# Down projections of two thirds of each feed-forward layer by Strassen's algorithm

## The chip, the core and the metric

The kernel runs on one core of one Trainium2 chip. A core has a matrix engine (TensorE, "PE" in the profile; its weight loads are listed apart as "PEld"), three engines for elementwise work (VectorE "DVE", ScalarE "ACT", GpSimd "POOL") and a queue that issues most transfers (SyncE, "SP"). Each engine runs its instructions in the order of its own queue, and waits for the others by semaphores. TensorE multiplies a 128x128 block of weights that stands in its array (the stationary operand) with a moving operand of up to 512 columns and adds the result into a bank of the accumulation memory (PSUM), which VectorE and ScalarE read. The other tiles lie in the on-chip memory SBUF, with 128 partitions.

The metric is the device time of the whole program in microseconds (us).

## The reference, cut to what matters

The model is a small decoder: one sequence of 512 tokens with 1024 features goes through an attention mixer, a feed-forward layer, a state-space mixer, a second feed-forward layer and a last norm. Everything is in float32. The change concerns only the last product of the feed-forward layers, `@ w_down`, whose inner dimension D_FF is 2816 = 22 x 128.

```python
D_MODEL = 1024
SEQ = 512
D_FF = 2816
FFN_CONV = 3
...
def conv_ffn(h, w_up, conv_w, conv_b, w_down):
    u = causal_depthwise_conv(h @ w_up, conv_w, conv_b)
    gate, up = u[..., :D_FF], u[..., D_FF:]
    return (jax.nn.silu(gate) * up) @ w_down
...
def reference(x, ...):
    cos, sin = rope_tables(x.shape[1])
    for i in range(DEPTH):
        h = rmsnorm(x, mix_norm_w[i])
        ...
        h = rmsnorm(x, ffn_norm_w[i])
        x = x + conv_ffn(h, ffn_w_up[i], ffn_conv_w[i], ffn_conv_b[i], ffn_w_down[i])
    return rmsnorm(x, final_norm_w)
```

## The kernel before

**Layout.** Features lie on the partitions and tokens along the free dimension. The residual stream is eight tiles `xr[0..7]` of 128x512 (L588). Weights arrive by transfer as float32, in units of 128x1024: eight 128x128 blocks side by side.

**Products in three parts.** A float32 product is made of three faster ones. Each operand is split into a high part, the value cast to the type fp32r, and a low part, the rest. `load_unit` (L116) does this for a unit of weights: SP issues the transfer into a tile `raw` (4 of them in turn, pool `wr`), ScalarE casts it to `hi` (L125) and VectorE subtracts to get `lo` (L126); there are five `hi` and five `lo` in turn (pool `wh`). `mm3` (L136) issues high x high, high x low and low x high into one bank, by `long_product` (L133), which calls the matrix product with the columns in the order that `in_turns` (L129) gives. So a unit of 8 blocks is 24 products of 512 columns.

**A feed-forward layer** (`ffn`, L610) goes over the 22 hidden tiles c in three parts, `FF_PARTS = ((0, 8), (8, 8), (16, 6))`. For each c it projects two units, gate and up (`project`, L146: 24 products each, into one of three banks "mm"), VectorE multiplies by the norm's factor `rbc` (L620), `conv` (L602) applies the three taps (one instruction of ScalarE, L603, and two of VectorE, L605), ScalarE applies silu (L624), and GpSimd multiplies the two (L627). The result is split for the down projection: ScalarE casts `g_h` (L629), GpSimd subtracts `g_l` (L630). The tiles `g_h`, `g_l` come from `high_low` (L81), eight of each in turn, so that a part fills them.

At the end of a part `down` (L263) computes what the part's hidden tiles add to the eight output tiles: for each output tile m it loads a unit of `wdn`, multiplies its blocks with the part's `g` tiles, and `add` (L639) adds the bank to `xr[m]` on VectorE (L640). The product with the last `g` tile of a part is put off: that of m = 0 and m = 1 until three blocks into m = 2, then by one output tile (`late`, `depth`). So the down stage can start while the last `g` is still being made.

**Order.** A planner orders the instructions of each engine at build time by a simulated clock. Within a `manual_schedule` block the named engines keep the order in which the code issues; the down stages are in such a block for TensorE. The last part of layer 1 ends in `finish` (L1059), which also does the last norm; its last two output tiles are made in halves of 256 tokens (L1106 to L1117), so the old kernel has 72 products of 256 columns there.

**Other tiles that the change touches.** Banks: "mm" 3, "aux" 3, "side" 2, each 128x512. SBUF tiles in turn: "a" 13, "us" 3, "tmp" 2, "sq" 2, and, used by the state-space mixer only, "xdt" 2, "yt" 2, "lm" 4, "ee" 2, "prev" 2. `_layout` (L1176) arranges the weights on the host before the launch; `wdn` is one unit per layer, part and output tile.

## Time and profile before

| | |
|---|---|
| median of 3 runs | 1626.8 us (1625.71 to 1626.92) |
| the profiled execution, its own time | 1626.55 us |
| its span, first to last instruction | 1624.6 us |
| mean granted TensorE clock | 0.999 |
| moved by DMA | 165.13 MB, mean 102 GB/s |
| matrix products | 8038 |

The page lists busy time of each engine, then 40 equal slices of the span, the DMA queues, the chain of work that ended last (followed back from the last instruction to what released each step), the costliest groups of instructions, and the DMA issues. A group's row reads: line, engine, operation, written tile <- read tiles, shapes, count | busy us, mean ns of one | idle time of the engine just before them, and what ended it. A row of the timeline or of the chain begins with the start in us from the span's start and the duration in us. A row of a table by stretches has the stretch, its length, then busy us and instruction count of PE, PEld, DVE, ACT and POOL, the granted clock, the DMA share and GB/s.

The span divides into these stages, by the chain in order of time: attention until about 474 us, its output projection until 503, feed-forward layer 0 until 852, the state-space mixer until about 1268, feed-forward layer 1 until the end at 1624.6. In each feed-forward layer the three parts are visible as stretches of up projections ("u") and of down projections ("wd", in the very last one "wz").

### The profile page before, as it was taken

To read this page: it belongs to the slowest core of one execution; us is meant where nothing else is said; L and a number is where in the kernel's file an instruction comes from. 1 tells how busy PE (TensorE), PEld (TensorE's weight loads), DVE (VectorE), ACT (ScalarE), POOL (GpSimd) and SP (SyncE) were. 2 spreads that over 40 slices of the span, in tenths; PEclk is the share of its full clock that TensorE was granted. 3 is DMA by queue.
4 is the path that set the end of the run, shared out by engine and by line. 5 is a ranking of instruction groups with operands and counts; after the bars stand their busy time and mean duration, and the time that the engine had idled before them with its cause. 6 is when DMAs were issued, how large, how long until landed. Compare 5 with 4: busy or idle time off the path is not lost.

```text
span 1624.6 us, 21067 instructions
## 1 busy us (share of the span) xinstructions
PE 1615.7 (99%) x8038; PEld 1382.9 (85%) x8038; DVE 1082.8 (67%) x1813; ACT 655.0 (40%) x965; POOL 418.6 (26%) x272
## 2 busy tenths in 40 slices
PE   9999999999999999999999999999999999999998
PEld 8888888888888888888887888888888888888887
DVE  6366665266647855764657899988897784574564
ACT  5233332333334532432445455544443442342343
POOL 0444453045402320220231222222111341121020
PEclk9999999999999999999999999999999999999999
DMA  7322222222224323223233433334332232332321
GB/s 259 98 80 83 78 91 80 96 85 79 78 78 134 113 91 105 103 81 117 81 101 104 148 108 115 100 100 127 114 126 90 93 104 91 104 104 91 104 78 52
DMA packets 53235, 165.13 MB, mean 102 GB/s; under 512 B 6224, under 2 KB 9680, under 8 KB 53136
## 3 DMA queue, kind: packets, MB, share of 16 engines
q1 hardware_dynamic: 52304, 163.01, 30.5%
q8 instruction: 63, 1.03, 0.3%
q10 hardware_dynamic: 832, 0.79, 0.1%
q14 instruction: 36, 0.29, 0.1%
HBM read 161.62 MB, written 2.16 MB: 101 GB/s over the span
## 4 chain that ended last, share of the span: by engine, by line
PE 99%; ACT 0%; DVE 0%; POOL 0%; POOLq 0%; DVEq 0%; issue 0%
PE u L134 29%; PE qk L134 16%; PE wd L134 12%; PE v L134 8%; PE xs L134 5%; PE z L134 5%; PE wso L134 5%; PE wo L134 3%; PE c L134 3%; PE b L134 3%; PE wz L134 2%; PE py L830 1%; PE pg L490 1%; PE pp L477 1%; PE po L485 1%; PE pf L838 1%
## 5 line engine op out<-in xcount | busy, mean ns | idle before, releaser
L134 PE MATMUL u<-xh,lo_u 128*128 128x512 f32 x704 | 268.9, 382 | 0.0
L134 PE MATMUL u<-xh,hi_u 128*128 128x512 f32 x704 | 268.8, 382 | 0.0
L134 PE MATMUL u<-xl,hi_u 128*128 128x512 f32 x704 | 266.3, 378 | 0.0
L627 POOL TENSOR_TENSOR au<-au,au 128x512 f32<-128x512 f32 x43 | 58.5, 1360 | 422.2 <-DVE au L605 396.6
L605 DVE SCALAR_TENSOR_TENSOR au<-usu,par,au 128x511 f32<-128x511 f32 (+1 forms) x176 | 159.4, 911 | 7.6 <-ACT au L603 2.9
L125 ACT CAST hi_u<-raw_u 128x1024 fp32r<-128x1024 f32 x88 | 91.1, 1044 | 168.4 <-PE u L134 95.6
L388 POOL TENSOR_TENSOR rotqk<-rotqk,sr 32x512 f32<-32x512 f32 x48 | 88.2, 1837 | 250.2 <-DVE rotqk L387 239.8
L134 PEld LDWEIGHTS u<-xl,hi_u 128*128 128x128 f32 x704 | 131.7, 187 | 24.5
L134 PEld LDWEIGHTS u<-xh,lo_u 128*128 128x128 f32 x704 | 131.7, 187 | 24.0
L134 PEld LDWEIGHTS u<-xh,hi_u 128*128 128x128 f32 x704 | 131.7, 187 | 21.8 <-issue 0.4
L134 PE MATMUL qk<-xh,hi_qk 128*128 128x512 f32 x384 | 148.6, 387 | 0.0
L134 PE MATMUL qk<-xh,lo_qk 128*128 128x512 f32 x384 | 147.1, 383 | 0.0
L134 PE MATMUL qk<-xl,hi_qk 128*128 128x512 f32 x384 | 145.6, 379 | 0.0
L126 DVE TENSOR_TENSOR lo_u<-raw_u,hi_u 128x1024 fp32r<-128x1024 f32 x88 | 113.8, 1299 | 29.9 <-ACT hi_u L125 29.9
L620 DVE TENSOR_TENSOR usu<-u,rbc 128x512 f32<-128x512 f32 x88 | 60.3, 690 | 93.1 <-PE u L134 86.4
L640 DVE TENSOR_TENSOR xr<-xr,wd 128x512 f32<-128x512 f32 x40 | 27.3, 688 | 116.9 <-PE wd L134 116.9
L125 ACT CAST hi_qk<-raw_qk 128x1024 fp32r<-128x1024 f32 x48 | 50.3, 1047 | 130.3 <-PE qk L134 69.3
L134 PEld LDWEIGHTS qk<-xh,lo_qk 128*128 128x128 f32 x384 | 71.8, 187 | 13.3
L134 PEld LDWEIGHTS qk<-xl,hi_qk 128*128 128x128 f32 x384 | 71.9, 187 | 12.8
L389 POOL TENSOR_TENSOR qk<-qk,rotqk 32x512 f32<-32x512 f32 x48 | 81.5, 1698 | 3.8
L125 ACT CAST hi_wd<-raw_wd 128x1024 fp32r<-128x1024 f32 (+1 forms) x48 | 46.1, 972 | 88.7 <-PE wd L134 55.6
L134 PEld LDWEIGHTS qk<-xh,hi_qk 128*128 128x128 f32 x384 | 71.9, 187 | 11.2
(647 smaller groups left out, 3768.5 us busy)
## 6 DMA issues: line engine op xcount, KB each, us to landing
raw_u<-in_wup SPq DMA_DIRECT2D x88, 512.0 KB, 3.3
raw_qk<-in_wqk SPq DMA_DIRECT2D x48, 512.0 KB, 3.3
raw_wd<-in_wdn SPq DMA_DIRECT2D x32, 512.0 KB, 3.2
raw_xs<-in_win SPq DMA_DIRECT2D x16, 512.0 KB, 3.3
raw_z<-in_win SPq DMA_DIRECT2D x16, 512.0 KB, 3.4
lm<-rows SPq DMA_DIRECT2D x32, 256.0 KB, 5.4
raw_wso<-in_wso SPq DMA_DIRECT2D x16, 512.0 KB, 3.3
raw_v<-in_wv SPq DMA_DIRECT2D x12, 512.0 KB, 3.5
```

The costliest lines, as they stand in the source:

```text
L125: SC.copy(hi[:, s], raw[:, s])
L126: low.tensor_tensor(lo[:, s], raw[:, s], hi.bitcast(F32)[:, s], op=ALU.subtract)
L134: T.matmul(in_turns(dst), w, in_turns(x), start=first, stop=last)
L388: G.tensor_tensor(rot[R, :], rot[R, :], sr[R, :], op=ALU.mult)
L389: G.tensor_tensor(at(t)[R], at(t)[R], of(rot)[R], op=ALU.add)
L477: T.transpose(pp[:, b * P : (b + 1) * P], pr[:, b * P : (b + 1) * P], ident)
L485: T.matmul(po[:, ii], v0[h][:, b * P : (b + 1) * P], pts[i][:, (b - i + 1) * P : (b - i + 2) * P], start=b == max(i - 1, 0), stop=b == i,)
L490: T.matmul(pg[:, ii], vt[g, half][i][:, es], pts[i][:, (g + 1) * P : (g + 2) * P], start=g == 1, stop=g == 2,)
L605: V.scalar_tensor_tensor(dst[:, j:], src[:, : S - j], col(c_w + taps - 1 - j), dst[:, j:], op0=ALU.mult, op1=ALU.add,)
L620: V.tensor_tensor(us, p, rbc, op=ALU.mult)
L627: by.tensor_tensor(ab[1], ab[0], ab[1], op=ALU.mult)
L640: V.tensor_tensor(xr[m], xr[m], p, op=ALU.add)
```

## The change

For the first two parts of each feed-forward layer (16 of 22 hidden tiles) the down projection is made by Strassen's algorithm in Winograd's form. A 2x2 block product takes two output tiles (rows), two hidden tiles (inner) and two halves of 256 tokens (columns). It is made of seven block products instead of eight, with sums of blocks ahead of them and sums of results behind.

- `gated` is the old inner loop for one hidden tile, as a function, up to the product of gate and up.
- `split_first` and `split_second` take the hidden tiles in pairs (an even c and the next). With the halves H0, H1 of the pair's two tiles they form the four operands that the algorithm needs beside the tiles themselves, on GpSimd, and split each into high and low. The tiles for those come from "lm", "ee", "prev", "xdt" and "yt". A part of 8 hidden tiles gives four pairs.
- `load_sevens` loads, for two output tiles and the four pairs, the four kinds of weight blocks (four transfers of 128x512), forms the four sums of blocks on GpSimd, and splits all seven kinds: three tiles of 1024 columns and one of 512.
- `down_by_sevens` runs four passes in a part, each for two output tiles. A pass has seven block products (`products`: 4 pairs x 3 matrix products of 256 columns, 84 in all), in a fixed order on TensorE. They go into four banks, three of which get a second block product on top of the first after a copy or sum of the first was taken. The results are added into the halves of the two residual tiles, by VectorE and twice by GpSimd.
- At the end of such a part the up projections and the gate of the next hidden tile (`held`) are issued ahead of the down stage.
- The third part (6 hidden tiles) uses `down` or `finish` as before.
- On the host, `wdn` keeps the third part only, and `wds` holds the blocks of the first two in the order of the four kinds.

```diff
+    def gated(layer, c):
...
+        SC.activation(ab[0], ab[0], AF.Silu)
+        by = V if layer == 1 and c == NFF - 1 else G
+        by.tensor_tensor(ab[1], ab[0], ab[1], op=ALU.mult)
+        return ab[1], by
+
+    H0, H1 = slice(0, 256), slice(256, 512)
+
+    def split_by(by, high, low, src):
+        SC.copy(high, src)
+        by.tensor_tensor(low, src, high.bitcast(F32), op=ALU.subtract)
...
+    def split_first(c, ga):
+        y = t2(f"y{c}", "a", 13, lp)
+        G.tensor_tensor(y[:, H0], ga[:, H1], ga[:, H0], op=ALU.subtract)
+        h, l = high_low(f"g{c}")
+        split_by(G, h[:, H0], l[:, H0], ga[:, H0])
+        split_by(G, h[:, H1], l[:, H1], y[:, H0])
+        return y, (h, l)
+
+    def split_second(c, ga, gb, y, j, fourth):
+        x = t2(f"x{c}", "a", 13, lp)
+        G.tensor_tensor(x[:, H0], gb[:, H1], y[:, H0], op=ALU.subtract)
+        G.tensor_tensor(y[:, H1], gb[:, H0], x[:, H0], op=ALU.subtract)
+        G.tensor_tensor(x[:, H1], gb[:, H1], ga[:, H1], op=ALU.subtract)
...
+        split_by(G, xhl[0][:, H0], xhl[1][:, H0], x[:, H0])
+        split_by(G, *f, y[:, H1])
+        b = split_whole(c, gb, G)
+        split_by(G, xhl[0][:, H1], xhl[1][:, H1], x[:, H1])
+        return xhl, f, b
+
+    def load_sevens(src, name):
...
+        def split_weights(r, t):
+            n = r.shape[-1]
+            hi, lo = (wh.tile([P, 1088], F32R, tag=k, name=f"{k}{t}_{name}")[:, 0:n] for k in ("hi", "lo"))
+            split_by(V, hi, lo, r)
+            return hi, lo
+
+        a, b, c = (raw(t) for t in "abc")
+        q = t2(f"q_{name}", "a", 13, lp)
+        W0, W1 = slice(0, 512), slice(512, 1024)
+        dma(a[:, W0], src[:, 0:512])
+        dma(q, src[:, 512:1024])
+        dma(b[:, W1], src[:, 1024:1536])
+        dma(c[:, W0], src[:, 1536:2048])
+        G.tensor_tensor(a[:, W1], q, b[:, W1], op=ALU.add)
+        G.tensor_tensor(b[:, W0], a[:, W1], a[:, W0], op=ALU.subtract)
+        G.tensor_tensor(c[:, W1], c[:, W0], b[:, W0], op=ALU.subtract)
+        G.tensor_tensor(q, a[:, W0], q, op=ALU.subtract)
+        return [split_weights(r, t) for r, t in ((a, "a"), (b, "b"), (c, "c"), (q, "d"))]
+
+    def down_by_sevens(layer, part, pairs):
+        n = f"wd{layer}{part}"
+        for mp in range(KD // 2):
+            a, b, c, d = load_sevens(A["wds"][(layer * 2 + part) * 4 + mp], f"{n}{mp}")
+            r1, r3, r2, r4 = (
+                (side_bank if i == 1 else aux_bank)(f"{n}{mp}r{i}")[:, 0:256] for i in range(4)
+            )
+            top, low = xr[2 * mp], xr[2 * mp + 1]
+            kept_sums = t2("kept", "tmp", 2, lp)
+            sums = t2("sums", "sq", 2)
+            s1, s5, u, w = kept_sums[:, H0], kept_sums[:, H1], sums[:, H0], sums[:, H1]
...
+            products(r1, a, 0, lambda x, f, g0, g1: halves(g0, H0), True)
+            SC.copy(s1, r1)
+            products(r3, a, 4, lambda x, f, g0, g1: halves(g0, H1), True)
+            SC.copy(s5, r3)
+            products(r2, b, 0, lambda x, f, g0, g1: halves(x, H0), True)
+            V.tensor_tensor(u, s1, r2, op=ALU.add)
+            G.tensor_tensor(top[:, H1], top[:, H1], u, op=ALU.add)
+            products(r4, b, 4, lambda x, f, g0, g1: f, True)
+            V.tensor_tensor(low[:, H0], low[:, H0], r4, op=ALU.add)
+            products(r1, c, 0, lambda x, f, g0, g1: halves(g1, H0), False)
+            V.tensor_tensor(top[:, H0], top[:, H0], r1, op=ALU.add)
+            products(r3, c, 4, lambda x, f, g0, g1: halves(g1, H1), False)
+            V.tensor_tensor(top[:, H1], top[:, H1], r3, op=ALU.add)
+            G.tensor_tensor(low[:, H1], low[:, H1], s5, op=ALU.add)
+            products(r2, d, 0, lambda x, f, g0, g1: halves(x, H1), False)
+            V.tensor_tensor(w, s1, r2, op=ALU.add)
+            low3 = low.rearrange("p (h t) -> p h t", h=2)
+            V.tensor_tensor(low3, low3, w.unsqueeze(1).to_broadcast([P, 2, 256]), op=ALU.add)
+
     def ffn(layer, done):
+        held = None
         for part, (c0, cn) in enumerate(FF_PARTS):
...
             for c in range(c0, c0 + cn):
...
+                g, by = held if c == c0 and held else gated(layer, c)
+                gs.append(g)
+                if part == len(FF_PARTS) - 1:
+                    pairs.append(split_whole(c, g, by))
+                elif c % 2 == 0:
+                    first = split_first(c, g)
+                else:
+                    y, g0 = first
+                    x, f, g1 = split_second(c, gs[-2], g, y, len(pairs), fourth)
+                    pairs.append((x, f, g0, g1))
+            if part < len(FF_PARTS) - 1:
+                held = gated(layer, c0 + cn)
+                with tc.manual_schedule(engines={mybir.EngineType.PE}):
+                    down_by_sevens(layer, part, pairs)
+                continue
```

More of the change, by code (lines that the diff above doesn't have):

```diff
@@ new lines, in down_by_sevens, with products, halves @@
+    def down_by_sevens(layer, part, pairs):
[4 more added lines that the diff above has]
+                (side_bank if i == 1 else aux_bank)(f"{n}{mp}r{i}")[:, 0:256] for i in range(4)
+            )
+            top, low = xr[2 * mp], xr[2 * mp + 1]
+            kept_sums = t2("kept", "tmp", 2, lp)
+            sums = t2("sums", "sq", 2)
+            s1, s5, u, w = kept_sums[:, H0], kept_sums[:, H1], sums[:, H0], sums[:, H1]
+            def products(dst, weights, at, operand, begin):
+                for j, pair in enumerate(pairs):
+                    mm3(
+                        dst, *weights, at + j, *(t for t in operand(*pair)),
+                        begin and j == 0, j == len(pairs) - 1, skip=True,
+                    )
+            def halves(t, h):
+                return [x[:, h] for x in t]
+            products(r1, a, 0, lambda x, f, g0, g1: halves(g0, H0), True)
[16 more added lines that the diff above has]
+            V.tensor_tensor(low3, low3, w.unsqueeze(1).to_broadcast([P, 2, 256]), op=ALU.add)
@@ L646, in ffn @@
+            if layer == 1:
+                finish(load, lambda c: pairs[c], cn)
                 return
             with tc.manual_schedule(engines={mybir.EngineType.PE}):
-                down(f"wd{layer}{part}", load, range(KD), lambda c: (gh[c], gl[c]), cn, add, late=True)
+                down(f"wd{layer}{part}", load, range(KD), lambda c: pairs[c], cn, add, late=True)
     def ups(layer, some):
```

77 lines of the change are left out of this document (42 added, 35 removed).

## The prediction

> **What bounds the kernel now.** I read the page's busy table first, then the chain of work that ended last.
>
> ```profile
> PE 1615.7 (99%) x8038; PEld 1382.9 (85%) x8038; DVE 1082.8 (67%) x1813; ACT 655.0 (40%) x965; POOL 418.6 (26%) x272
> ...
> PE 99%; ACT 0%; DVE 0%; POOL 0%; POOLq 0%; DVEq 0%; issue 0%
> ```
>
> TensorE (PE) is both the busiest engine and, for 99% of the span, the chain itself. So a change gains what it takes off PE, and loses what it makes PE wait. The chain in order of time prices the stages that change:
>
> ```profile
> 588.36 42.24 PE wd L134 x192
> 630.60 84.48 PE u L134 x384
> 715.08 42.24 PE wd L134 x192
> ...
> 1349.98 42.24 PE wd L134 x192
> ...
> 1476.70 42.24 PE wd L134 x192
> ...
> 1582.30 29.97 PE wz L134 x162
> ```
>
> The reader is to see four down stages of 192 products, each 42.24 us, with no wait in them: 42.24/192 = 0.220 us for a 512-wide product, and the up projections have the same pace (84.48/384). These four stages, 168.96 us, are what the change rewrites. The last row mixes widths: 108 products of 512 and 54 of 256. At 0.220 the first take 23.76 us, so 6.21 us are left for the 54. The timeline of PE confirms it:
>
> ```profile
> 1605.89 0.27 PE L134 MATMUL wz<-g16h,hi_wd 128*128 128x256 f32 x1
> 1606.00 0.27 PE L134 MATMUL wz<-g16l,hi_wd 128*128 128x256 f32 x1
> ...
> 1610.01 0.28 PE L134 MATMUL wz<-g16h,hi_wd 128*128 128x256 f32 x1
> ...
> 1612.10 0.50 PE L247 MATMUL ss<-ones,ssum 128*128 128x1 f32 x4
> ```
>
> From the first 256-wide product to what follows the last is 1612.10 - 1605.89 = 6.21 us: **0.115 us each**, where half of 0.220 would be 0.110. The printed 0.27 is latency, as ends are modelled; the pace is in the starts.
>
> What the other engines do while PE is in a down stage:
>
> ```profile
> 588.36:630.60 42.24, 42.24 (x194) 35.90 (x193) 15.23 (x17) 9.35 (x11) 2.57 (x2) 1.00 0.26 88
> ```
>
> VectorE (DVE) works 15.23 us of 42.24, ScalarE (ACT) 9.35, GpSimd (POOL) 2.57 (third to fifth of the busy figures); the clock is 1.00. So there is much cover here, and the question is whether the change uses it up.
>
> **PE's own term.** A pass of the new code does two output tiles: seven block products of 4 pairs x 3 = 84 products of 256, for 2 x 24 = 48 of 512. 84 x 0.115 = 9.66 us instead of 48 x 0.220 = 10.56. There are 4 passes in a part, 2 such parts and 2 layers, so 16 passes: 1344 x 0.115 = 154.6 us for 168.96, **14.4 us less**. Seven for eight would be 12.5%, or 21 us; the narrow product gives a third of it back.
>
> **What the other engines get.** Prices of single instructions:
>
> ```profile
> L126 DVE TENSOR_TENSOR lo_v<-raw_v,hi_v 128x512 fp32r<-128x512 f32 x8 | 5.3, 684 | 0.0
> L1076 DVE TENSOR_TENSOR xr<-xr,wz 128x256 f32<-128x256 f32 x4 | 1.7, 420 | 3.7 <-PE wz L134 3.7
> L1096 POOL TENSOR_TENSOR ot<-xw,rbc 128x256 f32<-128x256 f32 x3 | 2.1, 729 | 1.4 <-ACT rbc L1114 1.4
> L125 ACT CAST hi_wd<-raw_wd 128x1024 fp32r<-128x1024 f32 x16 | 16.5, 1043 | 38.3 <-PE wd L134 24.7 <-PE u L134 13.6
> L629 ACT CAST g5h<-au 128x512 fp32r<-128x512 f32 x1 | 0.6, 617 | 0.0
> L225 ACT ACTIVATE sq<-xr 128x256 f32<-128x256 f32 x2 | 0.8, 418 | 1.8 <-DVE xr L1076 1.8
> ```
>
> and one stretch of the up stage in which DVE and POOL meet (from the timeline of all engines):
>
> ```profile
> 569.40 1.53 DVE L605 SCALAR_TENSOR_TENSOR au<-usu,par,au 128x511 f32<-128x511 f32 x2
> 571.08 1.29 POOL L627 TENSOR_TENSOR au<-au,au 128x512 f32<-128x512 f32 x1 [5.85 <-DVE au L605]
> ...
> 573.42 1.23 DVE L126 TENSOR_TENSOR lo_wd<-raw_wd,hi_wd 128x1024 fp32r<-128x1024 f32 x1 [0.17 <-ACT hi_wd L125]
> ...
> 573.82 0.81 ACT L603 ACTIVATE au<-usu,par 128x512 f32<-128x512 f32 x1
> 573.99 1.80 POOL L630 TENSOR_TENSOR g5l<-au,g5h 128x512 fp32r<-128x512 f32 x1 [1.62 <-ACT g5h L629]
> 574.66 2.47 DVE L605 SCALAR_TENSOR_TENSOR au<-usu,par,au 128x511 f32<-128x511 f32 x2
> ...
> 577.22 0.63 ACT L624 ACTIVATE au<-au 128x512 f32<-128x512 f32 x1 [2.59 <-DVE au L605]
> ```
>
> Per pass:
> - ACT: two casts of 1024 (2.09 us) become three, one of 512 and two bank copies of 256: 3 x 1.04 + 0.62 + 2 x 0.42 = 4.6 us of 9.66. Covered.
> - DVE: two low halves and two adds (2 x 1.23 + 2 x 0.69 = 3.8) become three low halves of 1024, one of 512, five operations of 256 and one of 512: 3.69 + 0.68 + 2.10 + 0.68 = 7.2 us of 9.66.
> - POOL: from nothing to four weight sums of 512 and two adds of 256: 4 x 1.28 + 2 x 0.73 = 6.6 us.
> - DMA: two loads of 512 KB become four of 256 KB, the same bytes. The trace's 256 KB loads land in
>
> ```profile
> raw_wd<-in_wdn SPq DMA_DIRECT2D x32, 512.0 KB, 3.2
> ...
> xr<-in_xt SPq DMA_DIRECT2D x8, 256.0 KB, 3.9
> ...
> xp<-in_xp SPq DMA_DIRECT2D x8, 256.0 KB, 5.4
> ```
>
> 3.9 to 5.4 us, and the four raw tiles let them start about a pass ahead; at a DMA share of 0.26 I cost them nothing. If that cover went, a pass would wait at most one landing, 5.4 us.
>
> Per pair of hidden tiles POOL goes from 2 products and 2 low halves (4 x 1.28 = 5.1 us) to 2 products, 1 low half of 512 and 9 operations of 256 (3.84 + 6.57 = 10.4 us of the pair's 4 x 24 x 0.220 = 21.1).
>
> **DVE and POOL do not add up as two engines.** In the stretch above a pair of DVE operations takes 1.53 us at 569.40 and 2.47 us at 574.66, where POOL runs; POOL's 1.29 us becomes 1.80 where DVE's low half is still running at its start. Laid end to end, the low half, POOL's operation and the two of DVE are 1.23 + 1.29 + 1.53 = 4.05 us; they took from 573.42 to 577.13, 3.71 us. So they ran one after the other, and each of the two hand-overs hid about 0.15 us. Operations with a bank as one input are free of it:
>
> ```profile
> L605 DVE SCALAR_TENSOR_TENSOR au<-usu,par,au 128x511 f32<-128x511 f32 (+1 forms) x176 | 159.4, 911 | 7.6 <-ACT au L603 2.9
> ...
> L620 DVE TENSOR_TENSOR usu<-u,rbc 128x512 f32<-128x512 f32 x88 | 60.3, 690 | 93.1 <-PE u L134 86.4
> ```
>
> the first group (two SBUF tiles) has a mean of 911 ns where 1.53/2 = 765 is its undisturbed price; the second, which reads a PSUM bank, stays at 690. The Trainium skill, page "SBUF — State Buffer", section "Who interferes with whom", says this as a rule: VectorE's second SBUF input comes through the read interface that GpSimd uses, and whichever starts second is blocked until the first is done. The trace agrees, except that about 0.15 us of each operation lies outside the block; by the rule alone, without that saving, the ledger below is at its upper end.
>
> So here is the ledger of that one shared resource for a part, from the start of the held unit's products (48 x 0.220 = 10.56 us ahead of the first pass) to the end of the fourth pass: 10.56 + 4 x 9.66 = **49.2 us**. Undisturbed durations:
> - rest of the last hidden tile: 2 x 0.77 + 1.28 + 6 x 0.73 + 1.28 = 8.5
> - held unit: 4 x 0.77 + 1.28 = 4.4
> - weights: 4 x (3 x 1.23 + 0.68 + 4 x 1.28) = 38.0
> - sums into the residual tiles: 4 x (0.68 + 2 x 0.73) = 8.6
> - weights of the next three up units: 3.7
>
> Together 63.2 us in 62 operations; if the two engines took turns at each, 61 hand-overs save 9.2 and 54.0 are left. Over the window by 4.8 to 14.0 us. Not due inside it are the held unit's 4.4 and two of the next units' low halves, 2.5. That leaves between 2.1 us to spare and 7.1 too many per part, before any weight work goes ahead into the up stage, which has little room itself: a pair there needs 4 x 1.23 + 8 x 0.77 + 10.4 = 21.5 undisturbed, 25 operations less 24 x 0.15 = 17.9, of 21.1. The value I take lies nearer the lower end, since a loaded pair of engines does take turns, as the stretch shows: **2 us of PE waits per part, 8 us in all**, where the ends are 0 and 28.
>
> **Edits I cost at nothing.** The held unit's 48 products only move: they stand ahead of the down stage instead of behind it, and their two weight loads go ahead of the first pass's four in SP's queue. They cover the last gate's chain: multiply by the norm 0.69, taps 0.81 + 1.53, gate 0.63, product 1.28, then difference, cast and low half (0.73 + 0.42 + 0.73) is 6.8 us undisturbed. Pair 3's difference operand is needed 10.56 us, two block products (24 x 0.115) and nine products (9 x 0.115) later, 14.4 us; with the cover gone it would be 6.8 us a part at most. Bank hand-back: the bank of the first block product is read by DVE behind whatever stands in its queue and is wanted again 24 products, 2.76 us, later. One low half held up by one POOL operation and then the read are 1.23 + 1.28 + 0.42 = 2.93, so in the bad case 0.2 us a pass, 3 us in all; it is counted in the 8. DVE's add of the third bank also waits for POOL's add to the same tile, which can stand behind a 1.28 us weight sum; behind it on DVE stand the last two sums of the pass, and the bank of the second block product is again wanted 2.76 us into the next pass.
>
> **Sum.** The profiled execution took 1626.55 us (span 1624.6, 1.95 around it; 0.25 under the median of 1626.8). 1626.55 - 14.4 + 8 = 1620.15, said as **1620**.
>
> **Rivals.**
> - *All hidden.* The shared resource has room after all, as at the ledger's lower end. 1626.55 - 14.4 = 1612. For it: 15.23 and 2.57 us of work in a 42.24 us stage now. Against: the ledger. Chance 0.20.
> - *Slower: the shared read path paces the passes.* Place: each pass's weight sums and low halves. A pass holds it 4 x 1.28 + 1.46 + 3.69 + 1.36 = 11.6 us undisturbed, 10.1 with ten hand-overs, against PE's 9.66. It decides from 0.90 us of wait a pass, that is 10.56 held (14.4/16); at 11.6 the passes take 16 x 11.6 = 186 us and the time is 1626.55 - 168.96 + 186 = 1643. At the middle of ledger and pass, with 20 us of waits, 1632. For it: a DVE queue that runs in order puts every block in front of what PE needs. Chance 0.23.
> - *The narrow products are slower on these tiles.* The 54 in the trace read other buffers, and the 18 after 1610.01 ran at 0.116. At 0.120 the term is 161.3 and the time 1626.55 - 168.96 + 161.3 + 8 = 1627, which is no change; at 0.126 the saving is gone even without a wait. That the change doesn't do what it says would look like this. The weight load bounds it from above: its row shows 0.19 us
>
> ```profile
> 1606.01 0.19 PEld L134 LDWEIGHTS wz<-g16h,lo_wd 128*128 128x128 f32 x1
> 1606.12 0.19 PEld L134 LDWEIGHTS wz<-g17h,hi_wd 128*128 128x128 f32 x1
> ```
>
> but the next one starts 0.11 us later, which excludes 0.19 as the pace. Chance 0.08.
> - *Only the bank hand-back bites*, 3 us: 1615. Chance 0.09.
>
> The Trainium skill, page "TensorE: Matmul & The Clock Gate", section "LDWEIGHTS (loading the stationary operand)", gives columns over 1.2 for a weight load in ns, 107 for 128 columns; by that a 256-wide product sits just at the load's own pace and narrower ones would gain nothing more. It agrees with 0.115, and changes nothing in the sum.
>
> **How the numbers follow.** The forecast, with 2 us a part and 1616 to 1625 around it, has the remaining 0.40. A measurement of this kernel can tell about 0.2%, 3.3 us, from no change: faster is below 1623.5. From the forecast 0.31 falls there and 0.09 into no change; all hidden and bank hand-back give 0.29 faster; the narrow-product rival 0.02, 0.04 and 0.02; the slower rival 0.03 into no change and 0.20 slower. That is 0.62 faster, 0.16 same, 0.22 slower. The range leaves out the end of the slower rival and the edge under all hidden: 1611 to 1637.
>
> **What would show it.** PE's down stage should be 336 products at 0.115 in rows of the chain, 38.6 us a part; any excess is waits, and the table of waits should name DVE's low halves or bank reads, behind POOL. DVE's 1024-wide low half should rise well over 1.23 us inside the passes and POOL's 512 over 1.28; if both stay there and PE shows no gap, all hidden was right. If the products' starts are over 0.118 apart without a wait named, the narrow product was mis-sized. PE gaps that end on a DMA, or on ACT, would mean that I costed a cover at nothing that was not there.

## The result, and the profile after

| | before | after |
|---|---|---|
| median of 4 runs each | 1626.55 us (1625.71 to 1626.92) | 1677.12 us (1676.58 to 1677.25) |
| ratio after / before, 95% interval | | 1.0311 [1.0293, 1.0329] |
| profiled execution, its span | 1626.55 us, 1624.6 us | 1676.58 us, 1674.8 us |
| mean granted TensorE clock | 0.999 | 0.987 |

The kernel became 3.1% slower; the forecast was 1620 us and its range ended at 1637. The page of the changed kernel, busy times and shares of the chain that ended last:

```profile
PE 1620.0 (97%) x8614; PEld 1406.4 (84%) x8614; DVE 1180.0 (70%) x1909; ACT 713.3 (43%) x1093; POOL 686.3 (41%) x496
...
PE 81%; DVE 7%; POOL 6%; issue 4%; ACT 2%; DMA 0%; POOLq 0%; DVEq 0%; ACTq 0%; SPq 0%
```

PE was 99% of the chain and is 81%: DVE, POOL and the steps between engines now take turns in it. Where, the table by stretches of the changed kernel shows; the stretches run from the last up projection ahead of each of the four new down stages to the end of the stage (columns as before: stretch, length, busy us and count of PE, PEld, DVE, ACT, POOL, granted clock, DMA share, GB/s):

```profile
598.50:654.50 56.00, 42.92 (x338) 41.60 (x338) 47.20 (x47) 23.96 (x34) 47.48 (x33) 0.91 0.33 96
739.30:791.80 52.50, 44.02 (x337) 43.13 (x338) 43.38 (x46) 22.97 (x30) 43.38 (x27) 0.90 0.36 102
1384.40:1442.40 58.00, 43.00 (x338) 41.91 (x338) 46.98 (x47) 25.78 (x37) 49.46 (x35) 0.88 0.32 92
1527.00:1579.50 52.50, 43.20 (x338) 41.96 (x338) 43.61 (x45) 22.87 (x30) 41.68 (x27) 0.93 0.35 102
```

Together 219.0 us, where the old stages took 4 x 42.24 = 169.0. The difference of 50.0 is the whole of the difference in span, 50.2. POOL goes from 2.57 us of 42.24 to 47.48 of 56.00, DVE from 15.23 to 47.20. The chain of the changed kernel has the last pass of each part as one piece:

```profile
644.94 9.65 PE wd003r L134 x84
...
782.28 9.64 PE wd013r L134 x84
...
1432.86 9.64 PE wd103r L134 x84
...
1569.92 9.66 PE wd113r L134 x84
```

84 products at 0.115 us, as forecast. So 16 passes need 154.2 us, and 219.0 - 154.2 = 65 us are waits. The same table, pass by pass in the first part of layer 0:

```profile
598.50:622.00 23.50, 13.29 (x85) 12.38 (x84) 16.72 (x14) 9.72 (x14) 22.35 (x16) 0.78 0.17 45
622.00:633.80 11.80, 10.04 (x85) 9.84 (x86) 11.77 (x13) 4.40 (x7) 11.44 (x8) 1.00 0.31 82
633.80:644.80 11.00, 9.88 (x86) 9.68 (x86) 9.43 (x10) 4.31 (x6) 8.77 (x7) 1.00 0.40 114
644.80:654.50 9.70, 9.70 (x87) 9.70 (x86) 9.29 (x14) 5.53 (x8) 4.92 (x4) 1.00 0.67 215
```

Two losses of different size. The first pass with the wait ahead of it takes 23.5 us instead of 9.64: 14 us. The second and third take 11.8 and 11.0. The fourth, in which hardly any of the part's weights are still to be prepared, takes 9.7. The longest waits of PE in the changed kernel (waited for: us in total, times, longest):

```profile
PE wd100r L134 <- ACT hia_wd L631: 9.0, 1, 9.0
PE wd000r L134 <- ACT hia_wd L631: 7.0, 1, 7.0
PE wd010r L134 <- DVE sums L723: 3.7, 1, 3.7
PE wd110r L134 <- ACT hia_wd L631: 2.9, 1, 2.9
PE wd010r L134 <- ACT hia_wd L631: 2.9, 1, 2.9
PE wd111r L134 <- DVE xr L726: 1.8, 1, 1.8
PE wd001r L134 <- DVE sums L723: 1.7, 1, 1.7
PE wd101r L134 <- DVE sums L723: 1.7, 1, 1.7
```

Four first passes wait for their own weights (`hia`, the cast of the first sum of blocks), for 7.0, 2.9, 9.0 and 2.9 us. The others wait for DVE's reads of banks (L723, L726). What stands behind the first kind is in POOL's timeline (a row's last bracket is the idle time before it):

```profile
595.12 1.28 POOL L625 TENSOR_TENSOR au<-au,au 128x512 f32<-128x512 f32 x1 [4.64 <-DVE au L605]
...
600.24 1.85 POOL L632 TENSOR_TENSOR x7l<-x,x7h 128x256 fp32r<-128x256 f32 x2
602.05 0.72 POOL L632 TENSOR_TENSOR f5l<-y,f5h 128x256 fp32r<-128x256 f32 x1
602.74 1.70 POOL L689 TENSOR_TENSOR rawa_wd<-q_wd,rawb_wd 128x512 f32<-128x512 f32 x1
```

The first sum of the first pass (L689) is made at 602.74, behind the gate product of the part's last hidden tile (L625) and the splits of that tile, though POOL had been idle for 4.64 us ahead of 595.12. And the durations of DVE's low halves, by line (duration ns min/median/max):

```profile
L632 DVE TENSOR_TENSOR loa_wd<-rawa_wd,hia_wd x16: 1219/2301/2308, 605.5 to 1563.9; 128x1024 fp32r<-128x1024 f32 x16
L632 DVE TENSOR_TENSOR lob_wd<-rawb_wd,hib_wd x16: 1224/1756/2296, 609.7 to 1566.1; 128x1024 fp32r<-128x1024 f32 x16
L632 DVE TENSOR_TENSOR loc_wd<-rawc_wd,hic_wd x16: 1211/1640/2290, 613.9 to 1568.5; 128x1024 fp32r<-128x1024 f32 x16
```

Undisturbed 1.21 to 1.22 us, in the median 1.64 to 2.30.

### The profile page after: what moved, and what is told of

The parts are those of the page before. It is cut to its first block, busy times and chain, and to the rows that moved or that the text cites. A ratio compares the mean times of both kernels' runs of the same rounds, so it can differ in the third digit from the quotient of the medians.

```text
span 1674.8 us, 22828 instructions
## 1 busy us (share of the span) xinstructions
PE 1620.0 (97%) x8614; PEld 1406.4 (84%) x8614; DVE 1180.0 (70%) x1909; ACT 713.3 (43%) x1093; POOL 686.3 (41%) x496
## 4 chain that ended last, share of the span: by engine, by line
PE 81%; DVE 7%; POOL 6%; issue 4%; ACT 2%; DMA 0%; POOLq 0%; DVEq 0%; ACTq 0%; SPq 0%
PE u L134 19%; PE qk L134 15%; PE v L134 8%; PE xs L134 5%; PE z L134 5%; PE wso L134 5%; DVE au L605 3%; PE wo L134 3%; PE c L134 3%; PE b L134 3%; PE wz L134 2%; PE wd L134 2%; POOL au L625 1%; PE py L953 1%; ACT au L603 1%
## 5 line engine op out<-in xcount | busy, mean ns | idle before, releaser
L605 DVE SCALAR_TENSOR_TENSOR au<-usu,par,au 128x511 f32<-128x511 f32 (+1 forms) x176 | 160.2, 918 | 50.2 <-ACT au L603 45.0
L134 PEld LDWEIGHTS u<-xh,hi_u 128*128 128x128 f32 x704 | 131.7, 187 | 21.8
L625 POOL TENSOR_TENSOR au<-au,au 128x512 f32<-128x512 f32 x43 | 58.8, 1368 | 220.2 <-DVE au L605 200.8
L126 DVE TENSOR_TENSOR lo_u<-raw_u,hi_u 128x1024 fp32r<-128x1024 f32 x88 | 122.2, 1393 | 34.5 <-ACT hi_u L125 34.4
L898 POOL TENSOR_TENSOR xdd<-xdt,dec 128x384 f32<-128x384 f32 x16 | 18.0, 1140 | 241.2 <-DVE xdt L897 241.2
L384 DVE TENSOR_TENSOR qk<-qk,cr 128x512 f32<-128x512 f32 x48 | 33.0, 688 | 72.7 <-PE qk L134 72.4
L126 DVE TENSOR_TENSOR lo_qk<-raw_qk,hi_qk 128x1024 fp32r<-128x1024 f32 x48 | 59.3, 1236 | 31.9 <-ACT hi_qk L125 31.9
```

The costliest lines, as they stand in the source:

```text
L126: low.tensor_tensor(lo[:, s], raw[:, s], hi.bitcast(F32)[:, s], op=ALU.subtract)
L134: T.matmul(in_turns(dst), w, in_turns(x), start=first, stop=last, skip_group_check=skip)
L384: V.tensor_tensor(at(t), of(p), of(cr), op=ALU.mult)
L605: V.scalar_tensor_tensor(dst[:, j:], src[:, : S - j], col(c_w + taps - 1 - j), dst[:, j:], op0=ALU.mult, op1=ALU.add,)
L625: by.tensor_tensor(ab[1], ab[0], ab[1], op=ALU.mult)
L898: G.tensor_tensor(v4(u[:, 0:384], 3), v4(t[:, 0:384], 3), b3(dec3[:, 0:3, heads[x]], 64), op=ALU.mult)
```

## The experiments

Each run's loss is given in two numbers, worked out from the starts of products in its trace: **first**, from the last product ahead of a part's first pass plus 0.22 to the start of the second pass, less 9.64; **later**, from there to the end of the fourth pass, less 3 x 9.64; all parts added. The first row is the changed kernel. The times of the change, e2, e5, e6, e10, e14 and e15 are medians of 4 to 11 executions, the others stand for one execution each. e1, e7, e8, e11 and e12 leave out the weight sums, so their results are not the reference's; they only show where time goes.

| run | first | later | time, us |
|---|---|---|---|
| the change | 53.7 | 11.4 | 1677.1 |
| e1_sums_out | 11.5 | -0.1 | 1622.7 |
| e2_own_tile | 28.3 | 14.2 | 1655.3 |
| e3_fresh_bank | 43.9 | 14.8 | 1669.9 |
| e5_sums_on_vector | 21.8 | 4.6 | 1645.1 |
| e6_two_on_vector | 20.1 | 10.6 | 1651.0 |
| e7_no_reads | 13.3 | -0.1 | 1624.7 |
| e8_no_sums_last_on_vector | 6.7 | 1.3 | 1619.1 |
| e9_tile_last_on_vector | 25.1 | 13.9 | 1651.2 |
| e10_vector_and_fresh | 13.2 | 3.6 | 1635.9 |
| e11_reads_for_nobody | 30.6 | 8.8 | 1652.5 |
| e12_copies_for_nobody | 43.8 | 0.1 | 1654.8 |
| e13_second_sums_behind | 38.8 | 11.2 | 1662.5 |
| e14_vector_fresh_behind | 14.8 | 3.4 | 1629.8 |
| e15_second_part_only (2 parts) | 1.3 | 2.1 | 1624.3 |
| e16_second_part_as_changed (2 parts) | 22.5 | 5.8 | 1651.0 |

With all four parts by sevens, a span less its two losses is 1609 to 1611 us, against 1624.6 - (169.0 - 154.2) = 1609.8 with no loss at all. So the two numbers hold all of it, but for three rows with sums on VectorE (e5, e6, e10), where 6 to 9 us more are lost, nearly all of it in up projections, in waits for VectorE's bank reads and at half clock behind them. Of the two runs with the second parts alone, e16 has 3 us more outside the two numbers. In e4, which isn't in the table, the added products hide where a pass would have begun.

### Without the weight sums

The four additions L689 to L692 are taken out and the blocks go unsummed into the splits, loaded whole.

```diff
-        dma(a[:, W0], src[:, 0:512])
+        dma(a, src[:, 0:1024])
...
-        G.tensor_tensor(a[:, W1], q, b[:, W1], op=ALU.add)
...
-        G.tensor_tensor(q, a[:, W0], q, op=ALU.subtract)
```

> The changed kernel without GpSimd's four weight sums in each of the 16 passes (the blocks are loaded unsummed, so the down projections are not computed as in the reference; the loads are 7/4 as large). Theory (GpSimd's sums cause the waits, by their place in its queue and by holding up VectorE): nearly all of TensorE's 50 us of waits and the 15 us at half clock go, about 1612 us, at most 1620. Rival 1 (the waits come from late transfers): they stay or grow with the larger loads, 1677 us or more. Rival 2 (VectorE's own order holds the banks, with or without GpSimd): the waits for banks inside the passes, 20 us, stay, about 1632 us.

1622.72 us, some 3 us over the theory's 1620: nearly all of the loss comes with the sums. The chain of this kernel has fourteen of sixteen passes in pieces of 9.63 to 9.65, among them

```profile
612.42 9.65 PE wd001r L134 x84
622.07 9.63 PE wd002r L134 x84
631.70 9.63 PE wd003r L134 x84
725.91 9.63 PE wd010r L134 x84
```

and its longest waits are

```profile
PE wd100r L134 <- POOL x7l L632: 3.4, 1, 3.4
PE wd000r L134 <- POOL x7l L632: 2.4, 1, 2.4
```

They stand in the first pass of the first part of each layer, and with the clock behind them they are the 11.5 us that are left. The table by stretches of e1 around the second one:

```profile
606.20:609.60 3.40, 3.40 (x19) 3.40 (x18) 3.36 (x5) 3.33 (x5) 1.96 (x2) 0.51 0.00 0
609.70:613.00 3.30, 3.30 (x31) 3.30 (x30) 3.30 (x4) 1.28 (x2) 3.30 (x3) 1.00 0.40 134
```

After the wait of 2.4 us the granted clock is 0.51 for 3.4 us, in which PE starts 19 products instead of some 31: 2.4 us of wait and 12 x 0.115 = 1.4 us of slow products are most of the 4.2.

PE waits for the low half of the last tile's difference `x`. It comes from a gate chain that is late. DVE's timeline of this kernel and of the one before, the norm's multiplication for the last hidden tile's second unit (`usu`):

```profile
593.88 0.68 DVE L618 TENSOR_TENSOR usu<-u,rbc 128x512 f32<-128x512 f32 x1
```

```profile
588.40 0.69 DVE L620 TENSOR_TENSOR usu<-u,rbc 128x512 f32<-128x512 f32 x1 [0.72 <-PE u L134]
```

Before, it followed its products at once (they end at 588.36). Without sums it stands 5.9 us behind them (they end 10.56 us, the held unit's products, ahead of the first pass, at 598.6), and the gate product comes at 598.47 instead of 592.19. ScalarE's timeline of e1 shows one reason:

```profile
589.53 0.41 ACT L631 CAST g6h<-au 128x256 fp32r<-128x256 f32 x1 [2.66 <-POOL au L625]
591.20 0.41 ACT L631 CAST g6h<-y 128x256 fp32r<-128x256 f32 x1 [1.26 <-POOL y L642]
591.51 0.81 ACT L603 ACTIVATE au<-usu,par 128x512 f32<-128x512 f32 x1
```

The first tap of the last tile's first unit (L603) has its input at 588.67, but stands in ScalarE's queue behind two casts for the tile before, which wait for GpSimd. How much of the 5.9 us this makes, and why only the first parts suffer from it, is not shown.

### Two symptoms: the banks and the clock

`e3_fresh_bank` gives the seventh product a bank that no earlier product of the pass holds; `e4_kept_busy` issues 30, 12, 38 and 12 products of 512 columns that nobody uses ahead of the four first passes, so that PE is not idle there.

```diff
+            r5 = mm_bank(f"{n}{mp}r5")[:, 0:256]
...
-            products(r2, d, 0, lambda x, f, g0, g1: halves(x, H1), False)
-            V.tensor_tensor(w, s1, r2, op=ALU.add)
+            products(r5, d, 0, lambda x, f, g0, g1: halves(x, H1), True)
+            V.tensor_tensor(w, u, r5, op=ALU.add)
```

> The changed kernel with the seventh block product of a pass in a bank of its own (one of the three that the down stage leaves unused), so that TensorE does not wait for VectorE's read of the third block product's bank. Theory (15 us of waits are TensorE waiting for that one read): about 1663 us (1659 to 1667). Rival (VectorE is late as a whole, so TensorE waits for its next read instead): 1672 us or more.

> The changed kernel with products of no use ahead of the first pass of each down stage (30 and 12 in layer 0, 38 and 12 in layer 1, of 0.22 us), which fill most of TensorE's idle time there. Theory (the granted clock falls to half because TensorE stands idle for 3 us and more, and 31 us of work at half clock cost 15 us): the clock stays at 1.00 there and the time is about 1663 us (1660 to 1667), though nothing useful is done earlier. Rival (the clock falls for another reason, or the half clock falls into waits and costs nothing): 1675 to 1679 us.

The bank is worth 7 us, between theory and rival, and the waits come back at the next pass's banks (`DVE sums L724`). That speaks for the rival's reason: VectorE is late as a whole, and the bank is only where PE notices it. Keeping PE busy gained nothing (1676.38 us), although the clock was kept up. The same stretches, first of the changed kernel and then of e4:

```profile
602.24:612.48 10.24, 5.74 (x25) 5.45 (x26) 5.73 (x4) 2.50 (x4) 9.55 (x7) 0.50 0.11 26
742.20:749.00 6.80, 6.03 (x27) 5.74 (x28) 2.65 (x3) 1.05 (x1) 6.37 (x4) 0.50 0.08 20
1387.30:1401.00 13.70, 6.40 (x28) 6.11 (x29) 7.68 (x7) 4.55 (x7) 12.65 (x10) 0.50 0.08 19
```

```profile
602.24:612.48 10.24, 8.04 (x48) 6.63 (x48) 5.79 (x4) 3.52 (x6) 9.55 (x8) 1.00 0.06 13
742.20:749.00 6.80, 4.35 (x33) 3.80 (x32) 2.35 (x2) 1.32 (x2) 6.67 (x4) 1.00 0.12 31
```

In these stretches the granted clock goes from 0.50 to 1.00, and PE waits for the weights all the same. The theory that slow products cost some 15 us fell.

### The tile of the fourth block

```diff
-        q = t2(f"q_{name}", "a", 13, lp)
+        q = t2(f"q_{name}", ("btok", "cb")[int(name[-1]) % 2], 1, lp)
```

> The changed kernel with the fourth raw weight tile q in one of two tiles that only the state-space mixer uses, instead of one of the 13 tiles of tag a. Theory (the first pass's sums stand late in GpSimd's queue only because q waits for a slot among the 13): the sums move ahead of the last tile's splits, 25 of the 30 us of waits at the start of the four down stages go, and the half clock after them, 15 us: about 1637 us (1630 to 1645). Rival (the shared read path has no room for the sums any earlier): the wait only moves, and less than 15 us are gained, 1662 us or more.

1655.34 us (ratio to before 1.0177 [1.0160, 1.0194]): 21.8 us of the loss hung on one tile. `q` shared the ring of 13 with the gate's tiles, and with it the first pass's sums stood behind the last tile. It was not the transfer that was late: in the changed kernel the four transfers of `q` were issued from 579.64 to 585 us and took 3.2 us in the median, while the first sum came at 602.74. So it is the order that the planner made with the shared ring; why it made it is not shown. With its own tile the four waits for `hia` are gone. The gain lies between the two expectations, because the sums of the second pass now go ahead of the last tile. POOL's timeline of this kernel:

```profile
593.58 2.01 POOL L689 TENSOR_TENSOR rawa_wd<-q_wd,rawb_wd 128x512 f32<-128x512 f32 x1 [0.20 <-issue]
...
602.45 1.73 POOL L691 TENSOR_TENSOR rawc_wd<-rawc_wd,rawb_wd 128x512 f32<-128x512 f32 x1
604.14 1.71 POOL L625 TENSOR_TENSOR au<-au,au 128x512 f32<-128x512 f32 x1
...
609.67 1.86 POOL L632 TENSOR_TENSOR x7l<-x,x7h 128x256 fp32r<-128x256 f32 x2
```

The last gate product (L625) is at 604.14 instead of 598.47 (e1), and PE waits for `x7l`.

### The sums on VectorE

```diff
-        G.tensor_tensor(a[:, W1], q, b[:, W1], op=ALU.add)
+        V.tensor_tensor(a[:, W1], q, b[:, W1], op=ALU.add)
...
```

with `q` in its own tile; all four sums in e5, the first two in e6.

> As e2_own_tile, with all four weight sums of a pass on VectorE instead of GpSimd. Theory (the passes are paced by the read path that GpSimd shares with VectorE's two-input operations): a pass holds it 5.1 + 4 x 0.69 + 1.46 = 9.3 us undisturbed, under TensorE's 9.65, and VectorE alone is then the tightest with 7.2 + 2.7 = 9.9 us: passes of 9.7 to 10.3 us, the last tile's splits on GpSimd no longer late, about 1622 us (1617 to 1630). Rival (VectorE's load and queue order are what TensorE waits for): more work there makes passes longer than 11 us, 1645 us or more.

> As e2_own_tile, with the first two weight sums of a pass on VectorE and the other two on GpSimd. Theory (shared read path): 5.1 + 1.4 + 2.6 + 1.46 = 10.5 us undisturbed per pass, less about 0.15 for each hand-over, so about 9.5: between e2_own_tile and e5_sums_on_vector in its passes, 10 to 10.6 us, and about 1630 us (1620 to 1640). Rival (VectorE's load): slower than e2_own_tile, over 1655 us.

1645.08 (ratio 1.0118 [1.0101, 1.0135]) and 1651.0 us (1.0151 [1.0136, 1.0166]): better than with the sums on GpSimd, but by less than expected; e5 came out where its rival had it, e6 between its two. In e5 the later passes lose 4.6 us instead of 14.2 although VectorE has four operations more a pass, and the first passes 21.8 instead of 28.3; some 6 us of this are lost again in up projections that wait for VectorE.

### What a sum does: it is waited for, and it reads

Three runs keep GpSimd about as busy in a pass (6.3, 5.1 and 4.9 us undisturbed) and change what it does. In e7, which goes on from e2, each sum is three fills of the same 512 columns, so that splits still wait for them but nothing is read (the products then use fills for sums):

```diff
-        G.tensor_tensor(a[:, W1], q, b[:, W1], op=ALU.add)
...
+        for t in (a[:, W1], b[:, W0], c[:, W1], q):
+            for _ in range(3):
+                G.memset(t, 0.0)
```

In e11, which goes on from e1, the reads are there and nobody waits for the result; e12 has two copies for each addition.

```diff
+        spare = t2(f"spare_{name}", ("btok", "cb")[int(name[-1]) % 2], 1, lp)
+        for t in (a, b, c, a):
+            G.tensor_tensor(spare, t[:, W0], t[:, W1], op=ALU.add)
```

> As e2_own_tile, but each weight sum on GpSimd is three fills of the same 512 columns with zero, which read nothing (so the weights are not the reference's). GpSimd stays busy with a similar amount of work at the same places. Theory (reads of GpSimd block VectorE's second read): VectorE's low halves of 1024 columns fall back from 1.84 us to about 1.23 in the passes, and passes 2 and 3 of a part take 9.6 to 9.9 us. Rival (GpSimd's own time or its place in the chain paces the passes): they stay at 11 us.

> The weights are used unsummed, as in the kernel of 1622.7 us (part of the computation left out), and GpSimd adds two halves of a loaded block into a spare tile four times a pass, 512 columns each: as many GpSimd additions of the same size as the sums, but no split, product or copy waits for their results. It separates the two things that a sum does: to be waited for, and to read two operands beside VectorE's subtractions. Theory (the reads): the 1024-wide low halves rise from 1.23 to about 1.7 us, second and third passes of each part go from 9.64 to 10.5 us or more, the last stay at 9.65, and the time is 1640 us or more. Rival (the chain of four sums that the splits wait for): passes of 9.64 to 9.8 us after the first, 1622 to 1627 us.

> As the run before, with eight GpSimd copies of 512 columns a pass in place of the four additions: one operand read each, the same number of columns read. Theory: it is an operation with two read operands that meets VectorE's, so the low halves stay near 1.23 us, the passes after the first at 9.64 to 9.8, and the time is 1622 to 1627 us. Rival: any read on GpSimd holds VectorE back: low halves over 1.4 us and over 1632 us.

The low half of `a` by line in e7, e11 and e12, and GpSimd's own operations of e7 and e12:

```profile
L632 DVE TENSOR_TENSOR loa_wd<-rawa_wd,hia_wd x16: 1217/1254/1785, 585.8 to 1511.5; 128x1024 fp32r<-128x1024 f32 x16
...
L691 POOL MEMSET rawa_wd<- x48: 516/526/539, 565.4 to 1502.7; 128x512 f32 x48
```

```profile
L632 DVE TENSOR_TENSOR loa_wd<-rawa_wd,hia_wd x16: 1211/1806/2314, 585.7 to 1539.9; 128x1024 fp32r<-128x1024 f32 x16
```

```profile
L632 DVE TENSOR_TENSOR loa_wd<-rawa_wd,hia_wd x16: 1212/1633/1777, 582.8 to 1539.8; 128x1024 fp32r<-128x1024 f32 x16
...
L692 POOL COPY spare_wd<-rawa_wd x64: 603/613/1612, 568.0 to 1555.4; 128x512 f32<-128x512 f32 x64
```

With fills GpSimd is busy for 12 x 0.526 = 6.3 us a pass, more than four undisturbed sums (5.1), and both engines run at their own pace: no later pass loses anything. So it is not GpSimd's time, nor being waited for alone, but its two-operand reading beside VectorE that stretches a pass. These reads alone, waited for by nobody, cost the later passes 8.8 us of e2's 14.2; the rest came only with both together, and no run splits it further. Of the 8.8, most stand in the third passes (10.9 to 12.2 us); the second took 9.6 to 10.3, less than the theory had. Copies cost them nothing (0.1), though the low half of `a` still takes 1.63 in the median. Of e12's two theories each was right in one part: any read holds VectorE back, as the rival had it, but eight short reads leave the passes their 9.64, and the time was lost in the first passes. The Trainium skill, page "SBUF — State Buffer", section "Who interferes with whom", says that a VectorE instruction with two inputs in SBUF contends with a GpSimd instruction that reads there, not with one that only writes; the three medians agree, 1.25 beside fills, 1.81 beside additions, 1.63 beside copies.

For the first passes the three runs do not part reads from place: the fills wait for fewer loads, and some of them stand earlier in the queue. That the copies lose more there (43.8 us) than the additions (30.6) is a matter of place: e12 has four waits for the low half of the fourth block product's operand (`f5l` and `f13l`, 14.0 us together) and e11 none. In layer 0 GpSimd makes `f5l` at 613.01, behind copies, the next gate product and an addition to the residual tile.

### The last pair on VectorE

```diff
+        by = V if j == 3 else G
-        G.tensor_tensor(x[:, H0], gb[:, H1], y[:, H0], op=ALU.subtract)
+        by.tensor_tensor(x[:, H0], gb[:, H1], y[:, H0], op=ALU.subtract)
...
```

(three differences and four low halves); in e8 on top of e1, in e9 on top of e2.

> The kernel without the weight sums (blocks loaded as they are, which leaves part of the computation out) took 1622.7 us, and all that its passes lost stood in the first pass of part 0 of each layer: 13.86 and 16.91 us instead of 9.65, in waits for the low half of the last tile's differences on GpSimd. Here the three differences and four low halves of each part's last pair are made on VectorE as well. Theory: these 4.2 + 7.3 us are the last tile's splits behind GpSimd's other work and nothing else; all sixteen first to last passes then take 9.6 to 9.9 us and the time is 1611 to 1613 us. Rival: VectorE, which also has the held unit's convolutions there, is as late with them: the first passes stay over 12 us and the time at 1619 us or more.

> The sums stay on GpSimd, q has a tile of its own, and the three differences and four low halves of each part's last pair are made on VectorE. The kernel with only q's own tile took 1655.3 us; its four first passes were 9.7, 3.5, 11.4 and 4.0 us over 9.65 and its second and third passes 11.0 to 12.1. Theory: the excess of the first passes is half or more due to the last tile's splits queued on GpSimd, that of the second and third passes to GpSimd's sums reading beside VectorE; so the first passes fall to 10 to 13 us, the second and third stay at 11 to 12, and the time is 1632 to 1642 us. Rival: the sums before the first pass then hold the first pass instead and the time stays at 1650 us or more.

e8 gave 1619.12 us: the wait for POOL's `x7l` turned into shorter ones for DVE's and for ScalarE's bank copy (1.8 us, twice). That is the rival's time: 11.5 us of loss became 8.0, and the first passes still took over 12 us. So the place of the last splits is the smaller part; the larger fits the late chain ahead of them, which no run removed. e9 gained 4 us, not 13 to 23, the rival again: with the sums ahead, the gate product itself is late (603.19 in its trace), and what follows it matters little.

### Only the order

In e13, e2 with the second pass's sums and splits issued behind the last split of the last tile:

```diff
+        with tc.issue_after(tail[0].ins) if name[-1] == "1" else nullcontext():
+            G.tensor_tensor(a[:, W1], q, b[:, W1], op=ALU.add)
...
```

> q in its own tile and all sums on GpSimd, as in the kernel of 1655.3 us, but the second pass's four sums and splits of each part are issued behind the last tile's splits instead of ahead of its gate product (in that kernel's trace GpSimd made them from 593.6 to 604.2 us and the gate product of the last tile at 604.1, 5.7 us later than in the kernel without sums). Theory: the first passes, 28.3 us over the pace together there, fall to about the 11.5 us that they lost without sums, the second pass gives back 2 to 4 us a part, and the time is 1642 to 1648 us. Rival: what is moved only holds the second pass instead, 5.7 us a part, and the time stays at 1652 us or more.

1662.53 us, 7 us worse: the rival's time, but not its place, as the later passes lost 3 us less and the first passes 10.5 us more. The gate product did come earlier (601.42 instead of 604.14), and PE's waits for the last pair's splits in the first passes fell from 17.9 to 13.8 us. But in the same passes it now waited 7.2 us for DVE's first bank sum (0.3 in e2), which in layer 0 stood behind low halves of 1.9 and 2.3 us. With the sums on GpSimd the work at a part's start was too long in both orders. It also corrects the reading of e2: the sums that go ahead of the last tile are not simply misplaced.

### Both together, and where it pays

> All that was learned together: q in a tile of its own, the sums and the last pair's splits on VectorE, and a bank of its own for the seventh product. From 1645.1 us (sums on VectorE): its first passes were 8.5, 3.2, 6.9 and 2.7 us over 9.65, its second and third passes 0.3 to 1.4. Theory: with the last splits off GpSimd's queue most of these 21 us go and the bank takes 2 to 3 more: 1622 to 1630 us, about the time of the kernel before; not below 1618, as VectorE has 10.4 us of work in a pass of 9.65 us. Rival: VectorE, now with all of it, is late as a whole, and the waits come back under other names: 1636 us or more.

> The kernel of 1635.9 us (own tile, sums and last splits on VectorE, a fresh bank) with the second pass's sums and splits behind the last tile's splits. Its first passes were 3.9, 2.1, 5.7 and 2.0 us over 9.65 and its gate product of the last tile came at 603.25 us against 598.47 without sums, behind VectorE's sums. Theory: the gate product comes back to 598 to 600 us, the first passes to 10 to 12.5 us, the second passes take 10.2 to 11: 1627 to 1632 us, no faster than the kernel before. Rival: VectorE now has both the last splits and the second pass's preparation in one stretch, and the second passes lose what the first gain: 1634 us or more.

1635.87 (ratio 1.0060 [1.0047, 1.0074]) and 1629.84 us (1.0023 [1.0014, 1.0033]). e10 ended at its rival's bound, and with its rival's reason: 7 of its 24 us of loss are in up projections, ahead of the passes, most of them in waits for VectorE:

```profile
PE u L134 <- DVE usu L618: 4.9, 3, 2.7
```

Once the sums are on VectorE, the order is worth 6 us, which it was not on GpSimd. e14's theory had the time and the gate product (599.45 us) right, but not the place of the gain: the waits of the up projections are gone, while the passes lose 18.2 us where e10's lost 16.8, and the first passes of the two first parts took 16.3 and 16.8 us, not 10 to 12.5. Of the 18.2 us, 13.7 stand in these two first passes. e15 goes on from e14 and makes the first part by the old `down` again; e16 does the same to the change as it was.

```diff
-            if part < len(FF_PARTS) - 1:
+            if part == 1:
                 held = gated(layer, c0 + cn)
```

> As the kernel of 1629.8 us (own tile, sums and last splits on VectorE, fresh bank, second pass's preparation behind the last tile's), but the first part of each layer goes by the old down projection and only the second by seven block products. In that kernel the first parts lost 6.6 and 7.1 us in their first passes, the second parts 0.1 and 0.9, and the passes behind them 0.0 to 1.5. Theory: the start of a first part is late because the layer's gate chain starts late there (the last tile's gate product came at 592.2 us before, four us behind its products, and at 598.5 without sums), and the second parts keep most of their 3.7 us gain each: 1626.1 - 7.3 + 2.9 = 1621.7 us, between 1620 and 1623. Rival: the loss is that of any part, and moves to the second parts' first passes: 1627 us or more.

> The change as it is, sums on GpSimd and q in the ring of 13, but in the second part of each layer only. Those parts lost 13.3 + 0.7 and 10.2 + 3.8 us there. Theory: the losses belong to each part by itself, so 1626.1 - 7.3 + 28 = 1647 us, 1640 to 1652. Rival: the second parts were late because of the first; alone they lose less than half, under 1635 us.

e15: 1624.34 us, ratio 0.9986 [0.9977, 0.9995], the one version with the whole computation that is not slower than the kernel before; the gain is 2.5 us, by the interval 0.8 to 3.7. Its chain is 91% PE. Expected were 1620 to 1623; the two parts lost 3.5 us instead of the 2.9 reckoned, the rest of the miss is not placed. e16: 1651.0 us, 28.3 us lost in two parts, as its theory had it. So the large losses belong to each part by itself; only what e14 still lost was special to the first ones. The price of a VectorE sum, from e14's timeline:

```profile
604.25 0.68 DVE L693 TENSOR_TENSOR rawa_wd<-q_wd,rawb_wd 128x512 f32<-128x512 f32 x1
```

A sum is 0.68 us on VectorE, 1.28 on an undisturbed GpSimd. And with the sums on VectorE the low half of `a` is back at 1.24 us in the median (e5), from 2.30 in the change.

## Why the prediction was wrong

- **PE's own term: right.** 9.64 to 9.66 us a pass where 9.66 stood; the 14.4 us are there in every run, under the waits.
- **Prices of single instructions: right undisturbed** (sums from 1.26, low halves from 1.21 us), and the contention that the forecast saw is the one that e7 and e11 show. (A pair in the up stage has 24 operations where the forecast counted 25; that moves its 17.9 us to 18.0 and nothing else.)
- **The step that failed: "2 us of PE waits per part, 8 us in all, where the ends are 0 and 28."** Measured were 65 us, 16 a part. The ledger compared a sum of durations with a window that began at the held unit's products, and took what did not fit as wait. The later passes alone lost 11.4 us in all; that this is near the 8 is luck, since the ledger's window also holds the start of the part. For that start, where 53.7 us went, it has no term of its own. There it matters which of the operations PE needs first, and they stand in queues that run in order: the last tile's product and splits, the first pass's sums and the second pass's.
- **"They cover the last gate's chain ... 6.8 us undisturbed"** of 14.4: failed for the first parts, even without sums. The chain begins late: 5.9 us in e1, which lost 4.2 and 7.3 us there and nothing in the second parts. As price of a lost cover the forecast named 6.8 us a part at most, which is the right size for that loss alone.
- **Weight work "ahead into the up stage", "four raw tiles":** no PE wait in the down stages ends on a transfer, as costed; GpSimd's first sum of a pass (L689) waits for one four times, 2.9 us in all. But the fourth block has no raw tile; it has a slot in the ring of 13, and with that slot the sums were put behind the last tile: 21.8 us (e2).
- **"Bank hand-back ... 3 us in all":** 18 us of waits are named after bank reads in the changed kernel, but a bank of its own took only 7 away (e3). What is behind them is the late VectorE: in e7, where GpSimd reads nothing for the sums, no wait in the passes ends on a bank read.
- **Clock:** taken as 1.00, was 0.987; in the change that cost no time by itself (e4), in the kernels with fewer waits a few us (e1).
- **Rivals.** The slower one, the shared read path, had the sign and half of the mechanism; its upper end of 1643 counted the passes only, so it could not reach 1677. No rival had the start of a part as its place. "All hidden" was not reached even without the sums: e8 comes to 1619. The narrow products were not slower.
- **What would show it** was rightly named: the low halves over 1.23, POOL's 512 over 1.28, bank reads in the table of waits. PE waits that end on ACT were to mean "a cover at nothing that was not there", and the two longest do (`hia`).

## What to carry to other kernels

When a stage is rewritten so that an idle engine gets preparation to do, write down for the stage's first step what PE needs in order, and which queue each piece stands in; a ledger of durations over the whole stage misses this, and here it missed five sixths of the loss. Give elementwise work to GpSimd beside VectorE where it reads nothing (the fills of e7) or where VectorE's second operand is a bank (the 690 ns of the forecast's rows); else count both at the sum of their times, and expect even copies to hold VectorE up (e12). Four sums cost less on a VectorE that was already busier. A buffer taken from a ring that others use can change the place that the planner gives to the work behind it, even when the transfer itself is early.

## What the runs showed of the hardware

- PE's granted clock fell to 0.50 in the waits of 7.0 and 9.0 us, but also behind 2.9 us (742.20:749.00 above) and behind 2.4 us (e1), for 3.4 to 13.7 us; behind the waits of 1.8 us of e8 it did not (mean clock 0.999 there). The length of one wait does not decide it: in e4 the clock was 0.50 in 1396.00:1399.40 behind waits of 0.5 and 1.5 us, and in 1546.20:1549.50 behind several of at most 1.8 us. The Trainium skill, page "TensorE: Matmul & The Clock Gate", section "HAM oscillation — how this bites in real kernels", has idle gaps over about 3.4 us as the bound; here shorter ones were enough.
- Whether half clock costs anything depends on what comes next: in the change the first pass was short of weights anyway, and products at full speed only waited longer (e4); in e1, where nothing else was late, one such stretch cost the time of about 12 products.
- Fills of 512 columns on GpSimd take 0.526 us and leave VectorE nearly undisturbed (low half of `a` 1.25 us in the median, 1.22 in e1). A copy of 512 takes 0.61, half of a two-operand addition's 1.28, and beside the copies of e12 the low half of `a` took 1.63 us in the median.
